# Sums of the down weights in a pool of their own, and down-stage buffers in pools by first use

## The chip, the cores and the metric

The kernel runs on one core of a Trainium2 chip. A NeuronCore has TensorE (PE: matmuls, results in PSUM), VectorE (DVE), ScalarE (ACT), GpSimd (POOL) and SyncE (SP); here SP issues every DMA, in one queue in order. Each engine works through its own instruction list in order and waits for others by semaphores: an instruction that waits holds up everything behind it on its engine. The metric is the device time of one execution in microseconds (us), the median of several runs.

## The reference, cut to what matters

One layer over 128 context and 2048 latent tokens (2176 in all, width 1024), in float32:

```python
h = rmsnorm(x, norm1) * (1 + scale1) + shift1
sc_b, sc_c, sc_x, q, k, v, o, g = split(h @ w_in)
y_sc = sc_b * conv3(sc_c * sc_x)                 # short convolution
h_m = mlstm_bidir(q, k, v, g) normed * sigmoid(o)
x = x + gate1 * (concat(y_sc, h_m) @ w_out)
h2 = rmsnorm(x, norm2) * (1 + scale2) + shift2
a, gg = split(conv3(h2 @ w_up))
x = x + gate2 * ((silu(gg) * a) @ w_down)        # D_FF = 2816
y = rmsnorm(x, final_norm)
```

`shift`, `scale` and `gate` come from `silu(c) @ w_mod`.

## The kernel before, in words

Each float32 product is made of three matmuls: a value is split into a rounded high part and the rest (`wh`, `wl` for weights; `hH`, `hL` for activations), and `wh*hH + wh*hL + wl*hH` is summed in PSUM. ScalarE makes the high part, VectorE or GpSimd the rest.

Tokens are cut into six blocks of up to 384 (`BL`); group BB is blocks 3 to 5 (384, 384, 256), group BA blocks 0 to 2. The stages, in the order of the code:

1. Modulation for `norm1` on TensorE (`mod_pe`), then value projection and gates of BB (`vg`), then k and q of BB (`heads`), then the short convolution of BB (`shortconv`). For each of its four `m` and each block it has three gemms of 24 matmuls: `wc`, whose result ScalarE copies to `cr` (L388); `wx`, which VectorE multiplies into `cr` (L391); ScalarE starts `yr` (L393), VectorE adds two taps (L398, L400); `wb`, which VectorE multiplies into `yr` (L404). Each gemm takes one of four PSUM tiles `acc`; the tile is free again when the copy or product has read it.
2. Beside it runs the generator `side`: statistics of BA, the rest of the modulation (`mod_dve`: 32 rows of 512 KB, each multiplied twice on VectorE, L515, added at L517) and `down_sums`. The last makes four sums of quarter blocks of `w_down` (Strassen-like: the down stage uses 7 products in place of 8) and stores them to DRAM (`wsD`). It has 8 steps; a step loads four tiles of 128 x 704 float32 (352 KB each, L546), does four VectorE operations (L550 to L553) and stores four tiles (L556). The tiles are `wm` of the pool `start`, 5 buffers, which `mod_dve` uses too.
3. The output gate of BB and the normalisation of BA. The pool `start` is closed here; the next pools on its side (`ml`, `gt`, later `mb`) lie on its bytes.
4. Value projection and gates of BA (`run(vg(BA, ...))`), then `gate_phase` in the pool `gt`, woven with k of BA; then the pool `mb` is opened and the mLSTM scan runs (`weave`), with the rest of the projections and the output projection as filling; then the up stage (two halves, 22 column pairs, seven products each, on the slots `t6, t0, t1, t5, t2, t4, t3` in that order); then the down stage.
5. The down stage opens two pools: `dw` (weights: `st` 2 buffers, `wh` and `wl` 6 each) and `db` (activations: `us` 2, `cur` one for each of six parts, `bh` and `bl` 3 each of three widths), and starts with the loads of `cur` (L1038), their split into `bh` and `bl` (L1066, L1067) and that of the first weights (L1024 to L1028); the products are L1137 to L1139.

What sets the order of the instructions: the code is written as if it were sequential, and a planner then issues, for each engine, the ready instruction that stands first in the code, by its own estimate of when things are ready. An instruction written late but ready early can go out early. Pools with `side="right"` are laid from the top of SBUF downward in the order in which they are opened; a pool that is opened on bytes of closed pools has to wait for them.

Sizes per partition, from the tile shapes: `wh` or `wl` or `st` of the down stage 3072 bytes; `bh`, `bl` or `cur` 4352, 4352 and 3264 for the three parts; `us` 4352.

Of the kernel before, what the change touches and what calls it, by code (L numbers as in the profile page):

```python
# [18 lines left out]
P = 128  # L19
# [38 lines left out]
def hymba_kernel(ctx: ExitStack, tc: tile.TileContext, I, O):  # L58
# [42 lines left out]
    def run(g, side=None, every=1):  # L101
        for i, _ in enumerate(g):
            if side and i % every == 0:
                next(side, None)
# [209 lines left out]
    with ExitStack() as ph1:  # L314
# [21 lines left out]
        def load_vg(j):  # L336
            return [load_w(I["w_vg"][j, kk], WN) for kk in range(2)]

        def vg(blocks, hs, ws):
            for b in blocks:  # L340
                hH, hL = hs[b]
                for j in range(2):
                    for c in chunks(b):
                        o = c * P - BL[b][0]
                        acc = acc_tile()
                        for k in range(KT):
                            w_h, w_l = (x[:, (k % 4) * 264:(k % 4 + 1) * 264] for x in ws[2 * j + k // 4])
                            a_h, a_l = hH[:, k, o:o + P], hL[:, k, o:o + P]
                            PE.matmul(acc[:, :264], a_h, w_h, start=(k == 0), stop=False)
                            PE.matmul(acc[:, :264], a_h, w_l, start=False, stop=False)  # L350
                            PE.matmul(acc[:, :264], a_l, w_h, start=False, stop=(k == KT - 1))
                        r = rq.tile([P, 2, 129], F32, name="rv", bufs=4)
                        G.memset(r[:, :, 128:129], 1.0)
                        S.activation(r[:, :, :P], acc[:, :256].rearrange("p (h d) -> p h d", h=2), AF.Copy)
                        Q.dma_start(vD[c][:, 2 * j:2 * j + 2], r)
                        V.tensor_add(gates[:, c, j * 8:(j + 1) * 8], acc[:, 256:264],
                                     bgate[:, j * 8:(j + 1) * 8])
                        yield
# [107 lines left out]
        with tc.tile_pool(name="start", bufs=1, side="right") as stp:  # L466
# [41 lines left out]
            def mod_dve():  # L508
                for mt in range(16, 48):
                    st = stp.tile([P, 1024], F32, name="wm", bufs=5)  # L510
                    Q.dma_start(st, I["w_modr"][mt - 16])
                    t = stp.tile([P, 2], F32, name="mt", bufs=2)
                    for v in range(2):
                        jk = pm.tile([P, 2, 512], F32, name="y")
                        V.scalar_tensor_tensor(jk.rearrange("p a b -> p (a b)"), st, 1.0, cB[:, v], op0=ALU.mult, op1=ALU.mult,  # L515
                                               accum_out=t[:, v:v + 1])
                    V.tensor_scalar(modT[:, mt, :], t, bmod[:, mt:mt + 1], None, op0=ALU.add)  # L517
                    if mt == 39:
                        affine(1, 0, KT)
                    yield  # L520
# [10 lines left out]
            def first_stats():  # L531
                for b in BA:
                    ss = squares(b, load_x(b, I["x"], xp, "xt", 2))
                    yield
                    inv_rms(ss, BL[b][1], rcol(b))
                    yield

            def down_sums():

                n = KH * P // 2  # L540
                for m in range(4):
                    for q in range(2):
                        t = []
                        for mm, o in ((m + 4, n * 2), (m + 4, 0), (m, 0), (m, n * 2)):
                            x = stp.tile([P, 1024], F32, name="wm", bufs=5)
                            Q.dma_start(x[:, :n], I["w_down"][mm][:, o + q * n:o + (q + 1) * n])  # L546
                            t.append(x[:, :n])
                        yield
                        a22, a21, a11, a12 = t
                        V.tensor_add(a22, a21, a22)  # L550
                        V.tensor_sub(a21, a11, a21)
                        V.tensor_sub(a11, a22, a11)
                        V.tensor_sub(a12, a12, a11)  # L553
                        yield
                        for i, x in enumerate((a22, a11, a21, a12)):
                            Q.dma_start(wsD[i, m][:, q * n:(q + 1) * n], x)  # L556

            late()
            side = chain(first_stats(), mod_dve(), down_sums())
            run(vg((3,), hs, ws), prep(4))  # L560
            run(vg((4,), hs, ws), prep(5))
            run(vg((5,), hs, ws))
# [7 lines left out]
                hs[b] = make_h(b, I["x"], 0)  # L570

        ml = phr.enter_context(tc.tile_pool(name="ml", bufs=1, side="right"))


        WG, EM, AC = range(3)
# [143 lines left out]
        class Sums:  # L719
# [5 lines left out]
            def load(self):  # L725
                self.k2, self.v2 = load2(ml, "k2", kD, self.c + 1, self.hp), load_v(self.c + 1, self.hp)
# [133 lines left out]
                    next(fill, None)  # L860


        run(vg(BA, hs, load_vg(0) + load_vg(1)))
        with tc.tile_pool(name="gt", bufs=1, side="right") as gt:
            gph = gate_phase()
            kh = heads(BA, hs, 16, kD, AF.Copy, 1.0)
            while True:
                try:
                    next(gph)
                except StopIteration as e:  # L870
                    cols, colc, decB = e.value
                    break
                next(kh, None)
                next(kh, None)
            run(kh)
        php.close()
        del pas[1]
        pm = phr.enter_context(tc.tile_pool(name="pm1", bufs=1, space=PSUM))
# [131 lines left out]
    CK = ((0, 4), (4, 8), (8, KH))  # L1010
    PN = 2 * NB
    with ExitStack() as ph3:
        dw = ph3.enter_context(tc.tile_pool(name="dw", bufs=6, side="right"))
        db = ph3.enter_context(tc.tile_pool(name="db", bufs=3, side="right"))
        pd = ph3.enter_context(tc.tile_pool(name="pd", bufs=6, space=PSUM))

        def weights_d(i, m):
            n = KH * P
            w = [I["w_down"][m][:, :n], wsD[0, m], wsD[1, m], I["w_down"][m + 4][:, n:], I["w_down"][m][:, n:],
                 wsD[2, m], wsD[3, m]][i]  # L1020
            ws = []
            for a, e in ((0, 6 * P), (6 * P, n)):
                st = dw.tile([P, 6 * P], F32, name="st", bufs=2)
                Q.dma_start(st[:, :e - a], w[:, a:e])  # L1024
                wh = dw.tile([P, 6 * P], F32R, name="wh")
                wl = dw.tile([P, 6 * P], F32R, name="wl")
                S.activation(wh[:, :e - a], st[:, :e - a], AF.Copy)
                V.tensor_sub(wl[:, :e - a], st[:, :e - a], wh[:, :e - a].bitcast(F32))  # L1028
                ws.append((wh, wl))
            return ws  # L1030
# [31 lines left out]

        def parts(x, c):
            n = (CK[c][1] - CK[c][0]) * NB
            bh, bl = (db.tile([P, n], F32R, name=f"{k}{c}") for k in ("bh", "bl"))
            S.activation(bh, x, AF.Copy)  # L1066
            V.tensor_sub(bl, x, bh.bitcast(F32))  # L1067
            return bh, bl
# [177 lines left out]
```

## Time and profile before

| | |
|---|---|
| median of 3 runs | 2571.15 us (2570.41 to 2572.16) |
| profiled execution: time, span | 2569.87 us, 2568.1 us |
| TensorE, VectorE, ScalarE, GpSimd busy | 96%, 64%, 43%, 22% of the span |
| mean granted TensorE clock | 0.985 |
| DMA | 444.60 MB, mean 173 GB/s |

The span is from the first to the last instruction; busy shares are of the span. A busy TensorE is not TensorE at its peak. In a row of the timeline the brackets at the end hold the idle time of the engine before the instruction and what ended it.

### The profile page before, as it was taken

The page shows a single profiled execution, that of the slowest core. Times are in us where ns is not written, and L with a number is a line of the kernel's source. Part 1 is how long each engine was busy: PE and PEld are TensorE (multiplying, and loading weights), DVE is VectorE, ACT ScalarE, POOL GpSimd, SP SyncE. Part 2 cuts the span into 40 slices and gives each one's busy share as a digit, 9 for nine tenths or more (in the row PEclk, how much of TensorE's full clock was granted, in tenths as well). Part 3 has the DMA queues.
Part 4 walks back from the last instruction along what each step waited for, and adds up shares of the span by engine and source line. Part 5 has one row for each costly group of instructions (what it writes and reads, how often), then busy time and mean ns, then how long its engine had stood idle before and what let it go on. Part 6 is the DMA issues. An engine that isn't in the chain of part 4 may idle for free.

```text
span 2568.1 us, 42559 instructions
## 1 busy us (share of the span) xinstructions
PE 2469.4 (96%) x16127; PEld 2364.4 (92%) x16127; DVE 1644.1 (64%) x2741; ACT 1112.4 (43%) x2035; POOL 567.0 (22%) x470
## 2 busy tenths in 40 slices
PE   8997999999999889999999999899999989999998
PEld 7997999999999889889999999788888889999998
DVE  3995432322356565778678666877777786687676
ACT  4511133322245554455455444655555554444342
POOL 2542223211134333422112111221221200000000
PEclk9998999999999999999999999999999999999999
DMA  8788623356467787785225222422222286767674
GB/s 282 252 266 287 217 83 121 129 175 184 128 192 242 244 250 239 243 280 172 73 74 180 82 82 82 138 107 83 92 98 83 82 255 213 243 208 226 186 217 134
DMA packets 281423, 444.60 MB, mean 173 GB/s; under 512 B 23282, under 2 KB 206722, under 8 KB 279554
## 3 DMA queue, kind: packets, MB, share of 16 engines
q1 hardware_dynamic: 281218, 441.88, 53.1%
q8 instruction: 127, 2.08, 0.3%
q14 instruction: 78, 0.64, 0.1%
HBM read 335.31 MB, written 106.48 MB: 172 GB/s over the span
## 4 chain that ended last, share of the span: by engine, by line
PE 64%; DMA 6%; DVE 5%; issue 2%; ACT 2%; POOL 1%; SPq 0%; DVEq 0%; ACTq 0%; POOLq 0%
PE pa L979 6%; PE pa L981 6%; PE pa L980 6%; PE d L1138 5%; PE d L1139 5%; PE d L1137 5%; PE acc L204 4%; PE acc L206 4%; PE acc L205 4%; PE pb L979 3%; PE pb L981 3%; PE pb L980 3%; PE pc L979 2%; PE pc L980 2%; PE pc L981 2%
## 5 line engine op out<-in xcount | busy, mean ns | idle before, releaser
L204 PE MATMUL acc<-hH,wh 128*128 128x384 f32 (+1 forms) x1536 | 515.8, 336 | 23.3 <-DVE cr L391 9.9
L206 PE MATMUL acc<-hH,wl 128*128 128x384 f32 (+1 forms) x1536 | 506.5, 330 | 0.0
L205 PE MATMUL acc<-hL,wh 128*128 128x384 f32 (+1 forms) x1536 | 506.3, 330 | 0.0
L1137 PE MATMUL d<-bh,wh 128*128 128x272 f32 x1232 | 357.3, 290 | 6.5 <-ACT bh L1066 6.5
L1138 PE MATMUL d<-bl,wh 128*128 128x272 f32 x1232 | 357.6, 290 | 0.7 <-DVE bl L1067 0.7
L1139 PE MATMUL d<-bh,wl 128*128 128x272 f32 x1232 | 357.8, 290 | 0.0
L979 PE MATMUL pa<-tH,wh 128*128 128x288 f32 (+1 forms) x1056 | 347.9, 329 | 3.9 <-DVE raw L993 1.9
L981 PE MATMUL pa<-tH,wl 128*128 128x288 f32 (+1 forms) x1056 | 346.3, 328 | 1.0 <-DVE wl L294 1.0
L980 PE MATMUL pa<-tL,wh 128*128 128x288 f32 (+1 forms) x1056 | 346.6, 328 | 0.0
L294 POOL TENSOR_TENSOR wl<-st,wh 128x512 fp32r<-128x512 f32 x132 | 184.6, 1399 | 700.0 <-ACT wh L293 656.0
L113 POOL TENSOR_TENSOR wl<-wst,wh 128x512 fp32r<-128x512 f32 (+1 forms) x160 | 235.7, 1496 | 467.6 <-ACT wh L110 455.5
L204 PEld LDWEIGHTS acc<-hH,wh 128*128 128x128 f32 x1536 | 292.6, 191 | 26.6 <-DVE cr L391 11.0
L205 PEld LDWEIGHTS acc<-hL,wh 128*128 128x128 f32 x1536 | 292.8, 191 | 0.0
L206 PEld LDWEIGHTS acc<-hH,wl 128*128 128x128 f32 x1536 | 292.2, 190 | 0.2 <-issue 0.2
L924 DVE SCALAR_TENSOR_TENSOR tt<-raw,fw,tt 128x127 f32<-128x127 f32 (+4 forms) x264 | 245.2, 949 | 4.8 <-ACT tt L930 3.8
L1137 PEld LDWEIGHTS d<-bh,wh 128*128 128x128 f32 x1232 | 233.4, 190 | 7.0 <-ACT bh L1066 6.9
L1138 PEld LDWEIGHTS d<-bl,wh 128*128 128x128 f32 x1232 | 233.6, 190 | 1.2 <-DVE bl L1067 1.0
L1139 PEld LDWEIGHTS d<-bh,wl 128*128 128x128 f32 x1232 | 233.5, 190 | 0.0
L979 PEld LDWEIGHTS pa<-tH,wh 128*128 128x128 f32 x1056 | 198.2, 188 | 20.9 <-ACT c L986 2.6
L981 PEld LDWEIGHTS pa<-tH,wl 128*128 128x128 f32 x1056 | 198.8, 188 | 17.0 <-DVE wl L294 1.4
L980 PEld LDWEIGHTS pa<-tL,wh 128*128 128x128 f32 x1056 | 198.5, 188 | 15.6
L293 ACT ACTIVATE wh<-s 128x512 fp32r<-128x512 f32 x176 | 110.8, 630 | 177.8 <-PE pc L980 96.8
(235 smaller groups left out, 4840.3 us busy)
## 6 DMA issues: line engine op xcount, KB each, us to landing
st<-in_w_up SPq DMA_DIRECT2D x88, 512.0 KB, 4.4
us<-uD SPq DMA_DIRECT2D x48, 544.0 KB, 4.8
wst<-in_w_in SPq DMA_DIRECT2D x48, 512.0 KB, 4.3
uD<-tt SPq DMA_DIRECT2D x44, 544.0 KB, 2.7
R<-nD SPq DMA_DIRECT2D x34, 512.0 KB, 5.5
wm<-in_w_modr SPq DMA_DIRECT2D x32, 512.0 KB, 4.8
wst<-in_w_out SPq DMA_DIRECT2D x24, 512.0 KB, 4.9
st<-wsD SPq DMA_DIRECT2D x32, 384.0 KB, 3.4
```

Source lines behind the costliest of these rows:

```text
L113: G.tensor_sub(wl[:, a:a + n // 2], st[:, a:a + n // 2], wh[:, a:a + n // 2].bitcast(F32))
L204: PE.matmul(acc[:, :n], w_h, hH[:, k, :n], start=(k == 0), stop=False)
L205: PE.matmul(acc[:, :n], w_h, hL[:, k, :n], start=False, stop=False)
L206: PE.matmul(acc[:, :n], w_l, hH[:, k, :n], start=False, stop=(k == KT - 1))
L294: (G if on_pool else V).tensor_sub(wl, a, wh.bitcast(F32))
L924: V.scalar_tensor_tensor(o, i, w, o, op0=ALU.mult, op1=ALU.add)
L979: PE.matmul(acc, wh[:, w], rh, start=(kk == 0 and i in (0, 1, 5)), stop=False, skip_group_check=True)
L980: PE.matmul(acc, wh[:, w], rl, start=False, stop=False, skip_group_check=True)
L981: PE.matmul(acc, wl[:, w], rh, start=False, stop=(kk == 3), skip_group_check=True)
L1137: PE.matmul(acc, wh[:, c], uh, start=(kk == 0), stop=False)
L1138: PE.matmul(acc, wh[:, c], ul, start=False, stop=False)
L1139: PE.matmul(acc, wl[:, c], uh, start=False, stop=(kk == KH - 1))
```

## The change

`down_sums` leaves the generator `side` and the pool `start`. It is written anew with a pool of its own, `dsp`, opened after `ml`: four tile names of two buffers each (22,528 bytes per partition), each step's loads written one step ahead of its sums. Its steps are taken one by one beside the value projection of BA, the gate phase and k of BA; `dsp` is closed ahead of `mb`. The loads, sums and stores are the same in number and size.

In the down stage `dw` and `db` become seven pools, opened in the order `dw0` (`st` 2, `wh` 2, `wl` 2), `db0` (`bh`, `bl` of the three widths), `db` (`us` 2, the six `cur`), `db1`, `db2`, `dw1`, `dw2`; weights and activation sets take turns over three pools where they took turns over the buffers of one. The sum of the bytes is the same.

```diff
--- before.py
+++ after.py
@@ -535,28 +535,8 @@
                     inv_rms(ss, BL[b][1], rcol(b))
                     yield
 
-            def down_sums():
-
-                n = KH * P // 2
-                for m in range(4):
-                    for q in range(2):
-                        t = []
-                        for mm, o in ((m + 4, n * 2), (m + 4, 0), (m, 0), (m, n * 2)):
-                            x = stp.tile([P, 1024], F32, name="wm", bufs=5)
-                            Q.dma_start(x[:, :n], I["w_down"][mm][:, o + q * n:o + (q + 1) * n])
-                            t.append(x[:, :n])
-                        yield
-                        a22, a21, a11, a12 = t
-                        V.tensor_add(a22, a21, a22)
-                        V.tensor_sub(a21, a11, a21)
-                        V.tensor_sub(a11, a22, a11)
-                        V.tensor_sub(a12, a12, a11)
-                        yield
-                        for i, x in enumerate((a22, a11, a21, a12)):
-                            Q.dma_start(wsD[i, m][:, q * n:(q + 1) * n], x)
-
             late()
-            side = chain(first_stats(), mod_dve(), down_sums())
+            side = chain(first_stats(), mod_dve())
             run(vg((3,), hs, ws), prep(4))
             run(vg((4,), hs, ws), prep(5))
             run(vg((5,), hs, ws))
@@ -570,6 +550,37 @@
                 hs[b] = make_h(b, I["x"], 0)
 
         ml = phr.enter_context(tc.tile_pool(name="ml", bufs=1, side="right"))
+        phd = ExitStack()
+        dsp = phd.enter_context(tc.tile_pool(name="dsp", bufs=2, side="right"))
+
+        def down_sums():
+
+            n = KH * P // 2
+            todo = [(m, q) for m in range(4) for q in range(2)]
+
+            def load(m, q):
+                t = []
+                for i, (mm, o) in enumerate(((m + 4, n * 2), (m + 4, 0), (m, 0), (m, n * 2))):
+                    x = dsp.tile([P, n], F32, name=f"a{i}")
+                    Q.dma_start(x, I["w_down"][mm][:, o + q * n:o + (q + 1) * n])
+                    t.append(x)
+                return t
+
+            t = load(*todo[0])
+            yield
+            for k, (m, q) in enumerate(todo):
+                nt = load(*todo[k + 1]) if k < 7 else None
+                yield
+                a22, a21, a11, a12 = t
+                V.tensor_add(a22, a21, a22)
+                V.tensor_sub(a21, a11, a21)
+                yield
+                V.tensor_sub(a11, a22, a11)
+                V.tensor_sub(a12, a12, a11)
+                yield
+                for i, x in enumerate((a22, a11, a21, a12)):
+                    Q.dma_start(wsD[i, m][:, q * n:(q + 1) * n], x)
+                t = nt
 
 
         WG, EM, AC = range(3)
@@ -860,7 +871,8 @@
                     next(fill, None)
 
 
-        run(vg(BA, hs, load_vg(0) + load_vg(1)))
+        dsums = down_sums()
+        run(vg(BA, hs, load_vg(0) + load_vg(1)), dsums)
         with tc.tile_pool(name="gt", bufs=1, side="right") as gt:
             gph = gate_phase()
             kh = heads(BA, hs, 16, kD, AF.Copy, 1.0)
@@ -872,7 +884,10 @@
                     break
                 next(kh, None)
                 next(kh, None)
-            run(kh)
+                next(dsums, None)
+            run(kh, dsums)
+        run(dsums)
+        phd.close()
         php.close()
         del pas[1]
         pm = phr.enter_context(tc.tile_pool(name="pm1", bufs=1, space=PSUM))
@@ -1010,20 +1025,26 @@
     CK = ((0, 4), (4, 8), (8, KH))
     PN = 2 * NB
     with ExitStack() as ph3:
-        dw = ph3.enter_context(tc.tile_pool(name="dw", bufs=6, side="right"))
-        db = ph3.enter_context(tc.tile_pool(name="db", bufs=3, side="right"))
+        def right(name, bufs=1):
+            return ph3.enter_context(tc.tile_pool(name=name, bufs=bufs, side="right"))
+
+        dw, bslot = [right("dw0", 2)], [right("db0")]
+        db = right("db")
+        bslot += [right("db1"), right("db2")]
+        dw += [right("dw1", 2), right("dw2", 2)]
+        wturn, bturn = count(), count()
         pd = ph3.enter_context(tc.tile_pool(name="pd", bufs=6, space=PSUM))
 
         def weights_d(i, m):
             n = KH * P
             w = [I["w_down"][m][:, :n], wsD[0, m], wsD[1, m], I["w_down"][m + 4][:, n:], I["w_down"][m][:, n:],
                  wsD[2, m], wsD[3, m]][i]
-            ws = []
+            ws, pool = [], dw[next(wturn) % 3]
             for a, e in ((0, 6 * P), (6 * P, n)):
-                st = dw.tile([P, 6 * P], F32, name="st", bufs=2)
+                st = dw[0].tile([P, 6 * P], F32, name="st")
                 Q.dma_start(st[:, :e - a], w[:, a:e])
-                wh = dw.tile([P, 6 * P], F32R, name="wh")
-                wl = dw.tile([P, 6 * P], F32R, name="wl")
+                wh = pool.tile([P, 6 * P], F32R, name="wh")
+                wl = pool.tile([P, 6 * P], F32R, name="wl")
                 S.activation(wh[:, :e - a], st[:, :e - a], AF.Copy)
                 V.tensor_sub(wl[:, :e - a], st[:, :e - a], wh[:, :e - a].bitcast(F32))
                 ws.append((wh, wl))
@@ -1062,7 +1083,8 @@
 
         def parts(x, c):
             n = (CK[c][1] - CK[c][0]) * NB
-            bh, bl = (db.tile([P, n], F32R, name=f"{k}{c}") for k in ("bh", "bl"))
+            pool = bslot[next(bturn) // 3 % 3]
+            bh, bl = (pool.tile([P, n], F32R, name=f"{k}{c}") for k in ("bh", "bl"))
             S.activation(bh, x, AF.Copy)
             V.tensor_sub(bl, x, bh.bitcast(F32))
             return bh, bl
```

## Rows read from the trace of the kernel before

**Rows 1.** The page: busy us of an engine, share of the span, instructions.
```profile
PE 2469.4 (96%) x16127; PEld 2364.4 (92%) x16127; DVE 1644.1 (64%) x2741; ACT 1112.4 (43%) x2035; POOL 567.0 (22%) x470
```
**Rows 2.** Waits of TensorE: who waited for whom, us in total, times, longest.
```profile
PE acc L204 <- DVE cr L391: 9.9, 3, 8.1
...
PE d L1137 <- ACT bh L1066: 6.5, 1, 6.5
```
**Rows 3.** Stretches: us from:to, length, busy of each engine, clock, DMA.
```profile
204.00:218.00 14.00, 6.20 (x36) 5.87 (x34) 4.49 (x6) 0.00 (x0) 0.00 (x0) 0.80 0.85 287
218.00:230.00 12.00, 7.84 (x34) 7.53 (x35) 5.25 (x8) 1.08 (x2) 0.00 (x0) 0.78 0.95 353
230.00:250.00 20.00, 18.70 (x118) 18.29 (x118) 11.68 (x16) 4.85 (x7) 6.50 (x5) 0.93 0.90 307
250.00:290.00 40.00, 39.08 (x247) 38.88 (x247) 18.02 (x24) 6.18 (x10) 10.68 (x8) 1.00 0.84 299
...
395.00:450.00 55.00, 53.42 (x416) 53.00 (x415) 12.81 (x36) 17.66 (x35) 17.75 (x28) 0.97 0.29 96
```
**Rows 4.** Timeline of VectorE, 196 to 341 us: start, duration, line, operation, tiles.
```profile
199.87 1.97 DVE L551 TENSOR_TENSOR wm<-wm 128x704 f32<-128x704 f32 x1
...
203.72 0.21 DVE L517 TENSOR_SCALAR modT<-mt,bmod 128x2 f32<-128x2 f32 x1
...
214.13 0.89 DVE L550 TENSOR_TENSOR wm<-wm 128x704 f32<-128x704 f32 x1 [9.41 <-DMA wm<-in_w_down]
...
217.71 0.55 DVE L391 TENSOR_TENSOR cr<-acc,cr 128x384 f32<-128x384 f32 x1
...
306.61 0.42 DVE L391 TENSOR_TENSOR cr<-acc,cr 128x256 f32<-128x256 f32 x1 [5.22 <-PE acc L206]
...
317.87 0.56 DVE L391 TENSOR_TENSOR cr<-acc,cr 128x384 f32<-128x384 f32 x1 [6.74 <-PE acc L206]
...
340.42 0.42 DVE L391 TENSOR_TENSOR cr<-acc,cr 128x256 f32<-128x256 f32 x1 [5.23 <-PE acc L206]
```
**Rows 5.** Timeline of TensorE, 188 to 219 us.
```profile
188.99 0.44 PE L204 MATMUL acc<-hH,wh 128*128 128x384 f32 x1 [0.34 <-ACT row L364]
...
218.32 0.69 PE L204 MATMUL acc<-hH,wh 128*128 128x384 f32 x1 [8.12 <-DVE cr L391]
```
**Rows 6.** Loads of line 546: duration ns min/median/max, first and last start.
```profile
L546 SPq DMA_DIRECT2D wm<-in_w_down x32: 327/397/1525, 188.6 to 275.7; - x32
```
**Rows 7.** Timeline of the DMA queue of SP, at four places.
```profile
290.05 0.31 SPq L637 DMA_DIRECT2D sm<-in_state_m  x1
...
496.71 0.82 SPq L886 DMA_DIRECT2D sf<-in_state  x2
...
2049.71 0.33 SPq L1024 DMA_DIRECT2D st<-in_w_down  x1
...
2063.75 0.38 SPq L1038 DMA_DIRECT2D cur<-uD  x1
```
**Rows 8.** DMA issues: count, KB each, median us from issue to landing.
```profile
wm<-in_w_down SPq DMA_DIRECT2D x32, 352.0 KB, 4.4
wsD<-wm SPq DMA_DIRECT2D x32, 352.0 KB, 2.7
```
**Rows 9.** Two more stretches, as in rows 3; the last number is GB/s.
```profile
220.00:224.00 4.00, 4.00 (x17) 4.00 (x17) 0.00 (x0) 0.00 (x0) 0.00 (x0) 0.67 1.02 404
...
2070.20:2076.00 5.80, 5.07 (x21) 4.76 (x22) 5.80 (x6) 5.27 (x6) 0.00 (x0) 0.50 1.04 329
```
**Rows 10.** Timeline of GpSimd, 196 to 202 us.
```profile
196.98 4.11 POOL L113 TENSOR_TENSOR wl<-wst,wh 128x512 fp32r<-128x512 f32 x2 [12.36 <-ACT wh L110]
```
**Rows 11.** Timeline of TensorE, the first matmul of the down stage.
```profile
2070.14 0.60 PE L1137 MATMUL d<-bh,wh 128*128 128x272 f32 x1 [6.47 <-ACT bh L1066]
```
**Rows 12.** Groups of lines 1027 and 1028: count, busy us, mean ns of one.
```profile
L1028 DVE TENSOR_TENSOR wl<-st,wh 128x768 fp32r<-128x768 f32 x56 | 53.7, 960 | 27.8 <-ACT wh L1027 27.3
L1027 ACT ACTIVATE wh<-st 128x768 fp32r<-128x768 f32 x56 | 47.3, 844 | 84.2 <-PE d L1138 46.7 <-DMA st<-in_w_down 20.0 <-DMA st<-wsD 12.1
```

## The prediction

> **What bounds the kernel now.** I read the page first: TensorE is busy for 2469.4 of 2568.1 us [rows 1], so only its idle places and its slow places can be won. Then its waits by releaser [rows 2]: the change can touch two of them, the gemms' wait for `cr` L391 (VectorE, 8.1 us at once) and the one wait of 6.5 us for `bh` L1066 at the start of the down stage. Then a table of stretches [rows 3]: between 204 and 290 us TensorE idles 7.80 + 4.16 + 1.30 + 0.92 = 14.2 us, with DMA up to 353 GB/s and a granted clock of 0.80 and 0.78 in the first two; between 395 and 450 us, where the change writes the sums, VectorE is busy for 12.8 of 55 us and DMA moves 96 GB/s.
>
> The cause of the first place stands in VectorE's order [rows 4]. The first block's convolution starts on TensorE at 188.99 [rows 5], and a gemm takes (218.32 - 8.12 - 188.99)/5 = 4.24 us, so the second gemm `wx` is ready at 197.5. Its product L391, which frees a PSUM tile, runs only at 217.71: in front of it stand the end of the modulation work (203.9) and the second step of `down_sums`, which waits 9.41 us for its loads. TensorE has four such tiles, goes three gemms further and stops at 210.2 for 8.1 us. What the whole episode costs: one `m` of the convolution takes 340.42 - 306.61 = 33.81 us, and from its first block to its third 340.42 - 317.87 = 22.55 [rows 4]; undisturbed, the last product would be due at 197.5 + 3 x 33.81 + 22.55 = 321.5, and it comes at 340.42. So 18.9 us are lost: 14.2 idle and 4.7 at the lower of the clock's two levels (1.2 GHz) after the idle stretches. That is all that moving the sums can win here.
>
> **The sums, part by part.** Removed from `start`: 32 loads and 32 stores of 352 KB [rows 8] and 32 VectorE operations of 0.89 us [rows 4] (28.5 us). The same number is added in `dsp`: no transfer and no operation goes away. What changes is where they stand and how many buffers they have (two sets of four for one set and a fifth).
>
> Where they will stand is the first choice. In the code they move from shortconv's last `m` (317.87) to the value projection (395 on). But the order of issue isn't the order of the code: the loads of `down_sums`, written some 120 us further down, go out from 188.6 on, as soon as `wm` buffers are free [rows 6]; and the load of `sm`, written in the gate phase behind the value projection, goes at 290.05 [rows 7], when `start` is let go. The new sums wait for nothing but the memory of `start`, whose last reader is now the modulation work. So I expect them not at 395 but right after that work: at 203.9 less the three sums that stood between its instructions (two of 0.89 and one of 1.97, which overlap their neighbours a little, so 3.5 [rows 4]), at 200.4, again beside the first blocks of the convolution, and with lower priority than it.
>
> Then the times. One step moves 8 x 352 KB = 2.88 MB, at 404 GB/s [rows 9] 7.1 us. Eight loads go out at once from 200.4; a lone load lands in 4.4 us [rows 8], so the first set is there at 205 and the first step ends at 205 + 3.6 = 208.6; the second set is there at about 209.4 and its step ends at 213. In the order of before two steps stand ahead of the first product, and I take two again: a third needs a store and a load (2.7 + 4.4 us) behind the first. The product then comes at 213.5 in place of 217.7, and TensorE stands 3.3 us in place of 8.1. Further on steps three to eight follow at 7.1 us each, two to a block: 14.2 us against 12.6 (3 x 4.2) of gemms, so the second and third block lose about 1 us each. That makes 5.3 us idle, with the clock's share as before (4.7/14.2) 7.1. The loads of `k2`, `v2` and `sb` (nine, some 1.2 MB, 3 us at 404 GB/s) now go out here too, as `start` is freed sooner; I add 2.4. Back: 9.5 us. Won: 18.9 - 9.5 = 9.4. The ends: nothing back (18.9 won), or each further step ahead of the first product costing 7.1 us.
>
> The queues that are passed: a load that waits for a store holds SP, and behind it stand `wst` and the `yD` stores; before, such waits were as many and what TensorE waited for was VectorE [rows 2], so nothing is counted. `mb` now waits for the last store from `dsp` too; its first load goes at 496.71 [rows 7], the sums end before 290 in my reckoning, and even from 395 on (23.1 MB, 57 us at 404 GB/s) they would end some 44 us ahead of it.
>
> The trace shows one thing more: the sum at 199.87 took 1.97 us beside a POOL operation [rows 10], where others take 0.89 [rows 4]. The Trainium skill (SBUF — State Buffer, Who interferes with whom) says why: a VectorE operation with two SBUF inputs contends with a GpSimd operation that reads SBUF. The row agrees. By that rule eight sums that all met POOL would put the first product 8 x 1.08 = 8.6 us later, and the stall would be near that of before: 2571, the end of rival 2 by another way. In 204 to 290 us POOL is busy for 17 of 86 us [rows 3], so I count two sums, inside the 2.4 above.
>
> **The down buffers.** By the shapes, the slots of the up stage and its pools lie from the top down: slot 6 (18,432 bytes), `fpool` (20,736), slot 0 (18,432), `fp` (30,720, to 88,320). Before, `dw` takes 43,008 and `db` the next 104,448. A new pool waits until all older pools under its whole range are free: `sf`, read from an input alone, goes out only at 496.71, when the gate tiles are done, though it shares no byte with them; only its pool does. So `st` goes at 2049.71, when the last gemm on slot 0 is done, and `cur` at 2063.75, when the last gemm of all is done [rows 7]. After: `dw0` (18,432) lies on slot 6 alone, 2.8 us sooner (five gemm stages lie between 2049.71 and 2063.75); `db0` (to 42,368) on `fpool` and slot 0; but `db` with `cur` (to 75,008) still lies on `fp`, whose last wh and wl are read by the last gemm. The chain from `cur` at 2063.75 over bh to the first gemm at 2070.14 [rows 11] stays. The second weights now wait for slot 4 (one stage before the end) and their conversions come nearer to bh and bl: I take +1 us. Bounds: -9.4 if `cur` were free at 2049.7 (the wait of 6.47 [rows 11], and half of the 5.8 us to 2076 at a clock of 0.50 [rows 9]); +3.6 for two conversions (0.84 on ACT and 0.96 on VectorE each [rows 12]) in front of bh and bl.
>
> **Sum.** -9.4 + 1 = -8.4 on the profiled execution's 2569.87 us (span 2568.1) = 2561.5; the median of the runs is 1.28 higher, so 2562.7, say 2563.
>
> The page DMA: Bandwidth & Descriptors of the Trainium skill (Where 436 GB/s comes from) gives about 358 GB/s as what binds between HBM and SBUF. The row of 404 doesn't agree. By the page a step would take 8.1 us and the estimate be about 2 us later, 2565.
>
> **Rivals.**
> 1. The stall goes wholly, because the sums run where they are written, in the 42 us that VectorE has free between 395 and 450. For it: nothing there would wait. Against it: the loads issued ahead of their place [rows 6, 7]. 2571 - 18.9 + 1 = 2553. Chance 0.14.
> 2. It stays: three steps stand ahead of the first product, 7.1 us more come back (16.6 of 18.9). For it: in the order of before VectorE already ran 20 us behind its due places (217.71 for 197.5 [rows 4, 5]), so what is due just after the product can as well be due before it. 2570. Chance 0.29.
> 3. Slower. With two sets the first loads need no store, so the planner can fit more steps into the same gap: from four steps ahead of the first product on, 9.5 + 14.2 = 23.7 us come back, more than was lost. Five make 30.8: +11.9 + 1, 2584. For it: all loads wait for one event now; against it: a set must be stored before its next load. Place: VectorE's queue before L391. Chance 0.14.
> 4. My forecast, 2558 to 2567: 0.43.
>
> Faster by over 0.2% (about what a measurement tells from no change here, 5.1 us) means below 2566.0: most of case 4 (0.36), all of case 1, a little of 2 (0.04): 0.54. Slower, above 2576.3: 0.11 of case 3 and 0.03 of 2: 0.14. Same: 0.32. The range leaves out half of case 1 and the far half of case 3: 2553 to 2578.
>
> **What would show it.** Right: sums on VectorE between 204 and 265, two steps ahead of the first L391, that at 212 to 215, TensorE idle between 204 and 290 for about 5 us in place of 14.2, `cur` within 0.5 us of the last up gemm. Wrong: sums after 395 (case 1), three or more steps ahead of L391 (2 and 3), `cur` issued before the last gemm, or a change of over 3 us between 300 and 2040 us, where I count nothing.

## The result and the profile after

Before 2570.52 us (median of 16 runs), after 2577.58 us (16 runs): ratio 1.0031, 95% interval 1.0021 to 1.0040. The change makes the kernel slower, by 7 us between the medians and by 8.0 us (5.4 to 10.3 of 2570) by the ratio; 2563 was forecast. The profiled execution of the changed kernel (2571.69 us, span 2569.9) is the lowest of its 16 runs, so its span stands only 1.8 us above the one before, and the loss has to be read in its stage.

Line numbers have moved: the loads of the sums are L565, the sums L575 to L579, their stores L582; L391 and L404 are as before. Waits of TensorE (who waited for whom: us in total, times, longest), to be held against [rows 2]:

```profile
PE acc L204 <- DVE cr L391: 15.2, 4, 9.0
...
PE d L1159 <- ACT bh L1088: 6.7, 1, 6.7
```

The wait for L391 was to shrink and has grown from 9.9 to 15.2 us; the wait for `bh` is unchanged. The same stretches as in [rows 3] (length, busy PE, PEld, DVE, ACT, POOL, clock, DMA share, GB/s):

```profile
204.00:218.00 14.00, 6.64 (x38) 6.31 (x37) 6.06 (x7) 0.00 (x0) 0.00 (x0) 0.85 0.99 356
218.00:230.00 12.00, 9.46 (x49) 9.14 (x50) 6.71 (x10) 1.08 (x2) 0.00 (x0) 0.75 0.91 333
230.00:250.00 20.00, 13.26 (x73) 12.76 (x72) 9.22 (x9) 2.87 (x4) 6.68 (x4) 0.83 0.75 245
250.00:290.00 40.00, 37.02 (x234) 36.62 (x233) 19.22 (x30) 6.65 (x10) 8.34 (x6) 1.00 0.79 270
```

TensorE idles 7.36 + 2.54 + 6.74 + 2.98 = 19.6 us here; before it was 14.2. The first stretch is no worse than before; the third is the new loss (6.74 for 1.30), and there DMA moves less than before (245 for 307 GB/s), so it isn't the transfers that are short of room. VectorE, in order of time (start, duration, line, operation, tiles, idle before and what ended it), beside [rows 4]:

```profile
202.60 0.23 DVE L517 TENSOR_SCALAR modT<-mt,bmod 128x2 f32<-128x2 f32 x1
...
208.51 0.89 DVE L575 TENSOR_TENSOR a<-a,a 128x704 f32<-128x704 f32 x1 [5.48 <-DMA a<-in_w_down]
211.91 0.89 DVE L576 TENSOR_TENSOR a<-a,a 128x704 f32<-128x704 f32 x1 [2.50 <-DMA a<-in_w_down]
...
215.01 0.89 DVE L575 TENSOR_TENSOR a<-a,a 128x704 f32<-128x704 f32 x1 [0.36 <-DMA a<-in_w_down]
...
219.03 0.55 DVE L391 TENSOR_TENSOR cr<-acc,cr 128x384 f32<-128x384 f32 x1
...
224.66 0.89 DVE L575 TENSOR_TENSOR a<-a,a 128x704 f32<-128x704 f32 x1 [3.04 <-DMA a<-in_w_down]
...
235.14 0.89 DVE L575 TENSOR_TENSOR a<-a,a 128x704 f32<-128x704 f32 x1 [6.47 <-DMA a<-in_w_down]
...
238.43 1.98 DVE L578 TENSOR_TENSOR a<-a,a 128x704 f32<-128x704 f32 x1
241.88 1.95 DVE L579 TENSOR_TENSOR a<-a,a 128x704 f32<-128x704 f32 x1
...
249.33 0.89 DVE L575 TENSOR_TENSOR a<-a,a 128x704 f32<-128x704 f32 x1 [5.04 <-DMA a<-in_w_down]
...
266.34 0.89 DVE L575 TENSOR_TENSOR a<-a,a 128x704 f32<-128x704 f32 x1 [9.66 <-DMA a<-in_w_down]
...
286.87 0.89 DVE L575 TENSOR_TENSOR a<-a,a 128x704 f32<-128x704 f32 x1 [3.77 <-DMA a<-in_w_down]
...
348.15 0.42 DVE L391 TENSOR_TENSOR cr<-acc,cr 128x256 f32<-128x256 f32 x1 [5.23 <-PE acc L206]
```

Two steps stand ahead of the first product, as forecast, but that product runs at 219.03, later than before (217.71). From the third step on each waits for its loads (3.04, 6.47, 5.04, 9.66 ...), and in each of the first six blocks a product, L391 or L404, stands behind such a step. TensorE's first wait is no shorter than before ([rows 5]: 8.12 us):

```profile
219.64 0.69 PE L204 MATMUL acc<-hH,wh 128*128 128x384 f32 x1 [9.00 <-DVE cr L391]
```

The last product, L391 at 348.15, comes 7.7 us later than before (340.42): here the loss is seen. Of the 7.7 us 1.3 stand at the first product (219.03 for 217.71); the rest arises behind it. The third step is level with that of before, the eighth is 9.5 us later; the rows of before:

```profile
224.89 0.89 DVE L550 TENSOR_TENSOR wm<-wm 128x704 f32<-128x704 f32 x1 [5.24 <-DMA wm<-in_w_down]
...
277.38 1.58 DVE L550 TENSOR_TENSOR wm<-wm 128x704 f32<-128x704 f32 x1 [2.16 <-DMA wm<-in_w_down]
```

The DMA queue of SP says why the loads are late:

```profile
187.45 0.90 SPq L365 DMA_DIRECT2D qD<-row  x2
202.86 0.81 SPq L565 DMA_DIRECT2D a<-in_w_down  x2
203.77 0.38 SPq L365 DMA_DIRECT2D qD<-row  x1
204.19 0.43 SPq L108 DMA_DIRECT2D wst<-in_w_in  x1
204.66 0.48 SPq L565 DMA_DIRECT2D a<-in_w_down  x1
...
238.78 0.33 SPq L565 DMA_DIRECT2D a<-in_w_down  x1
244.31 0.32 SPq L405 DMA_DIRECT2D yD<-yr  x1
244.72 1.36 SPq L565 DMA_DIRECT2D a<-in_w_down  x3
```

SP issues nothing between 188.35 and 202.86: the first load of the new pool waits for the last reader of the whole pool `start`, and all else waits behind it; before, the sums' loads went out one by one from 188.6 [rows 6]. Later the queues of SP and VectorE hold each other: at 238.78 one load of a step goes out, the other three stand behind a `yD` store until 244.31, that store waits for its product L404 on VectorE, and L404 stands behind sums there.

The down stage: `cur` is issued at 2066.13, 0.06 us after the end of the last up gemm (its last matmul starts at 2065.67 and takes 0.40), as before, and the first matmul waits for it as in [rows 11]:

```profile
2066.13 5.16 SPq L1059 DMA_DIRECT2D cur<-uD  x6
```
```profile
2072.77 0.59 PE L1159 MATMUL d<-bh,wh 128*128 128x272 f32 x1 [6.71 <-ACT bh L1088]
```

### The profile page after: what moved, and what is told of

Same layout as the page of the kernel before. It is cut to its first block, busy times and chain, and to the rows that moved or that the text cites. A ratio compares the mean times of both kernels' runs of the same rounds, so it can differ in the third digit from the quotient of the medians.

```text
span 2569.9 us, 42547 instructions
## 1 busy us (share of the span) xinstructions
PE 2469.0 (96%) x16127; PEld 2364.7 (92%) x16127; DVE 1648.1 (64%) x2741; ACT 1112.4 (43%) x2035; POOL 561.2 (22%) x470
## 4 chain that ended last, share of the span: by engine, by line
PE 62%; DMA 7%; DVE 6%; issue 2%; ACT 1%; POOL 1%; SPq 1%; DVEq 0%; POOLq 0%; ACTq 0%
PE pa L994 6%; PE pa L996 6%; PE pa L995 6%; PE d L1160 5%; PE d L1159 5%; PE d L1161 5%; PE acc L204 3%; PE acc L206 3%; PE acc L205 3%; PE pb L994 3%; PE pb L996 3%; PE pb L995 3%; PE pc L995 2%; PE pc L994 2%; PE pc L996 2%
## 5 line engine op out<-in xcount | busy, mean ns | idle before, releaser
L204 PE MATMUL acc<-hH,wh 128*128 128x384 f32 (+1 forms) x1536 | 517.2, 337 | 26.7 <-DVE cr L391 15.2
L995 PEld LDWEIGHTS pa<-tL,wh 128*128 128x128 f32 x1056 | 198.2, 188 | 15.4
```

The source lines that it names most:

```text
L204: PE.matmul(acc[:, :n], w_h, hH[:, k, :n], start=(k == 0), stop=False)
L995: PE.matmul(acc, wh[:, w], rl, start=False, stop=False, skip_group_check=True)
```

## The experiments

Each kernel was timed against the kernel before, interleaved on the same chip. "Last L391" is the start of the last product of the convolution in its profiled execution.

| kernel | ratio to before, 95% interval | that is, us of 2570 | last L391 |
|---|---|---|---|
| before | 1 | 0 | 340.42 |
| after | 1.0031 (1.0021 to 1.0040) | +8.0 | 348.15 |
| sums_only | 1.0023 (1.0006 to 1.0039) | +5.9 | 347.51 |
| down_only | 1.0000 (0.9987 to 1.0014) | 0.0 | 343.25 |
| one_set | 1.0040 (1.0025 to 1.0055) | +10.3 | 349.43 |
| before_held | 1.0015 (1.0003 to 1.0027) | +3.9 | 346.55 |
| sp_order | 0.9980 (0.9968 to 0.9992) | -5.1 | 334.01 |
| dve_order | 0.9958 (0.9947 to 0.9970) | -10.8 | 330.01 |
| paced | 0.9962 (0.9950 to 0.9974) | -9.8 | 330.07 |
| late | 0.9973 (0.9959 to 0.9987) | -6.9 | 322.92 |
| paced2 | 0.9940 (0.9926 to 0.9954) | -15.4 | 322.72 |
| before_ordered | 0.9936 (0.9922 to 0.9949) | -16.4 | 323.00 |
| db_first | 0.9982 (0.9968 to 0.9996) | -4.6 | 339.43 |
| paced2_dbf | 0.9908 (0.9890 to 0.9926) | -23.6 | 322.04 |

Where the sums stay in the convolution and `cur` isn't moved, the shift of the last product is the change of the time to within some 3 us. So much one execution differs from another: before, down_only and db_first have the same convolution, and their last products stand at 340.42, 343.25 and 339.43. What lies between that product and the first up gemm took 787.3 us before, 783.1 after, and 782.5 to 792.4 in the twelve others.

**Which part: sums_only and down_only.** In the first, `dw` and `db` are put back; in the second, the sums are.

> The changed sums, with the down stage's two pools as before. Theory (the whole loss of 7 us is the sums': VectorE's queue in order holds the convolution's products L391 and L404 behind sums that wait for loads, and the last product came 7.7 us later): about 2577.5 us, +7, with VectorE's last L391 of the convolution at about 348 us. Rival (the down pools lose it, the sums are neutral): 2570.5 us, no change from before.

> The sums as before, with the changed down-stage pools. Theory (the down pools change nothing: cur is still issued at the end of the last up gemm and the first down gemm waits 6.5 us for bh): 2570.5 us, within 1.5 of before. Rival (the down pools carry the loss): 2577.5 us, +7.

The sums carry the loss (+5.9, last product at 347.51, span 2575.6), the down pools carry nothing. Their interval of -3.3 to +3.6 us doesn't tell my +1 from 0.

**The sums where they are written: late.** The edit keeps an order of issue on a queue; it adds no wait for completion:

```diff
-                    Q.dma_start(x, I["w_down"][mm][:, o + q * n:o + (q + 1) * n])
+                    with tc.issue_after(vst[0]):
+                        Q.dma_start(x, I["w_down"][mm][:, o + q * n:o + (q + 1) * n])
```

(`vst[0]` is the latest `vD` store of the value projection.)

> The changed kernel, but each load of the sums is kept behind the latest vD store written before it on SP's queue, so that the sums run beside the value projection and gate phase of BA where they are written, after the convolution. Theory (the loss is the products' wait behind the sums in VectorE's queue during the convolution): no sums between 200 and 330 us, no stall of TensorE over 2 us there, the convolution's last L391 at 321 to 327 us instead of 348, and the time 2552 to 2558 us. Rival 1 (the sums hold VectorE's part of the value projection, the gates, as they held the products, and half comes back): 2562 to 2570 us. Rival 2 (the loss was not the order in the convolution): 2577 us.

VectorE's last product, and one of the windows where the sums now stand:

```profile
322.92 0.42 DVE L393 TENSOR_TENSOR cr<-acc,cr 128x256 f32<-128x256 f32 x1 [5.23 <-PE acc L206]
```
```profile
395.00:450.00 55.00, 47.45 (x352) 46.58 (x352) 27.33 (x71) 14.67 (x30) 4.45 (x12) 0.96 0.93 317
```

No wait of TensorE for anything is left between 204 and 350 us, and the last product comes at 322.92. So the undisturbed convolution ends there: before lost 17.5 us, after 25.2. But the time falls by 6.9 only, not by 17.5: in the new place TensorE is busy for 47.45 of 55 us where it was 53.42 [rows 3], with DMA at a share of 0.93. The longest of its waits there, one that before doesn't have, is for VectorE:

```profile
PE S L673 <- DVE mi L669: 4.9, 1, 4.9
```

These rows show only a part of what comes back: the profiled execution (2557.58 us) is the lowest of its 12 runs and 12.3 us below that of before. My expectation of 2552 to 2558 was wrong, its first rival right (2563.18).

**Order or traffic: paced, dve_order, sp_order.** The sums stay in the convolution, all of their 23 MB too; only the order of issue is set, in both queues or in one:

```diff
+        def behind(done, k):
+            return tc.issue_after(done[k]) if k > 0 or done is prod else ExitStack()
...
+                    with behind(yst, 2 * m + q - 1):
+                        Q.dma_start(x, I["w_down"][mm][:, o + q * n:o + (q + 1) * n])
...
+                with behind(prod, k):
+                    V.tensor_add(a22, a21, a22)
+                    V.tensor_sub(a21, a11, a21)
```

`yst` holds the `yD` stores and `prod` the products L404, both by block. The first `behind` is SP's order (paced, sp_order), the second VectorE's (paced, dve_order). Steps and blocks are counted from 0 here; the loads of steps 0 and 1 are left free, the others stand behind the store of block k-1.

> The changed kernel with the sums left in the convolution, the same traffic in the same stretch, but put in order by hand: the sums of step k stand in VectorE's queue behind the product L404 of block k, and the loads of step k behind the yD store of block k-1 on SP's queue, so that each load has a block (11.3 us) of lead. Theory (the loss is the order in VectorE's queue: a product behind a sum that waits): the convolution's last L391 at 322 to 326 us instead of 348, no wait of TensorE over 2.5 us between 205 and 340 us, 2552 to 2560 us (the lower end if nothing comes back later as it does when the sums stand at 379 to 474). Rival (the loss is the sums' 23 MB of traffic beside the convolution, which slows weights and stores whatever the order): last L391 at 335 us or later, 2568 to 2577 us.

> As the ordered version of the sums in the convolution, but only VectorE's order is set (sums of step k behind L404 of block k); SP's order stays the planner's. Theory (VectorE's queue is the place of the loss): nearly as good as with both, last L391 at 322 to 328 us, 2553 to 2562 us. Rival (SP's queue, in which a load that waits for a store holds weights and yD stores, carries half or more): last L391 at 335 us or later, 2566 us or more.

> Only SP's order is set (loads of step k behind the yD store of block k-1); VectorE's order is the planner's, which puts two steps ahead of the first product L391 as in the changed kernel, and later sums beside products. Theory (VectorE's queue): the first product stays at 217 to 219 us and TensorE's wait of 9 us with it, the later waits shrink or stay; 2566 to 2577 us. Rival (SP's queue): the time falls as far as with both orders, below 2560 us.

The traffic isn't the cause: with it in place, order alone turns +8.0 into -9.8. VectorE's order carries all of it (-10.8 alone); SP's alone gives 13.1 of the 17.8 us between after and paced (-5.1). What SP's order leaves is the first wait. In sp_order the first product still stands behind two steps, and of the 8.7 us that TensorE waits for such products between 190 and 350 us, 8.4 are the wait for this one:

```profile
219.85 0.55 DVE L393 TENSOR_TENSOR cr<-acc,cr 128x384 f32<-128x384 f32 x1
```
```profile
PE acc L204 <- DVE cr L393: 8.7, 2, 8.4
```

So the later waits go when either queue is put in order, and the first one only with VectorE's. The expectation for sp_order had this first wait right and the time wrong: 2563.60 us lies between the theory (2566 to 2577) and its rival (below 2560).

In paced and dve_order the last product (330.07, 330.01) is 7 us later than in the undisturbed case, and later than expected (up to 326 and 328); their times are 2560.45 and 2560.64. VectorE of paced shows what still stands ahead of the first product, and TensorE what it costs:

```profile
202.54 0.23 DVE L519 TENSOR_SCALAR modT<-mt,bmod 128x2 f32<-128x2 f32 x1
...
216.21 0.23 DVE L668 COPY mi<-sm 1x4 f32<-1x4 f32 x2 [13.24 <-DMA sm<-in_state_m]
216.35 0.54 DVE L393 TENSOR_TENSOR cr<-acc,cr 128x384 f32<-128x384 f32 x1
```
```profile
216.95 0.69 PE L204 MATMUL acc<-hH,wh 128*128 128x384 f32 x1 [6.96 <-DVE cr L393]
```

Two copies of four numbers, which the program has only in the gate phase, were issued ahead of the product, and they wait 13.24 us for a 32-byte load that stands on SP behind the eight loads of the sums.

**One set of buffers: one_set.** `bufs=2` of `dsp` becomes `bufs=1`.

> The changed kernel with one buffer of each of the four names in place of two. My prediction counted on the second set for a pace of 7.1 us a step, and the changed kernel makes 11.2 us. Theory (the pace is set by the transfers themselves and by SP's queue, 2.9 MB a step at some 260 GB/s, not by the buffers): a step every 11 to 13 us, 2574 to 2582 us. Rival (the second set carries the pace): a step every 15 us or more, the sums end after 320 us, 2585 us or more.

Slower than before by 10.3 us, which doesn't tell it from after (+8.0); its time, 2580.99 us, lies in the range of the theory. Its steps start at 209.4 to 305.5, some 13.7 us apart, where two sets made (286.87 - 208.51)/7 = 11.2. That is between the theory (11 to 13) and the rival (15 or more): the second set does shorten a step, but not to 7.1.

**The later start alone: before_held.** In the kernel before, one element of each tile of the first step is written by VectorE behind the last L517:

```diff
+                            if m + q == 0:
+                                with tc.issue_after(mod_end[0]):
+                                    V.memset(x[:, :1], 0.0)
                             Q.dma_start(x[:, :n], I["w_down"][mm][:, o + q * n:o + (q + 1) * n])
```

> The kernel before, in which the first four loads of the sums may not go out until the modulation work is done (a one-element write of their tile behind the last L517 on VectorE, about 203 us), as the new pool makes them wait in the changed kernel; before, they go out from 188.6 us. Nothing of pools or buffers is changed. Theory (what the change costs over before is this later start, since the sums keep their pace of 10.5 to 11 us a step and the products are tied to them): the last L391 of the convolution at 346 to 352 us instead of 340.4, 2576 to 2582 us. Rival (the cost lies in the new pool and its order, not in the start): last L391 at 341 us, 2570 to 2572 us.

```profile
190.72 0.91 SPq L365 DMA_DIRECT2D qD<-row  x2
205.53 0.81 SPq L551 DMA_DIRECT2D wm<-in_w_down  x2
```
```profile
226.12 0.55 DVE L391 TENSOR_TENSOR cr<-acc,cr 128x384 f32<-128x384 f32 x1
...
346.55 0.42 DVE L391 TENSOR_TENSOR cr<-acc,cr 128x256 f32<-128x256 f32 x1 [5.23 <-PE acc L206]
```
```profile
PE acc L204 <- DVE cr L391: 13.5, 1, 13.5
```

The same gap in SP's queue as after, and 3.9 us (0.8 to 6.9) of loss: in its direction as expected, in its size half. The 2576 to 2582 of the expectation would be +6 or more; the last product is in the expected range. But the loss stands in another place than after. Here it is one wait of 13.5 us for the first product, which comes at 226.12; after, with a second set of buffers, that product came at 219.03, 1.3 us later than before, and the loss arose behind it. So a later start costs the kernel before 3.9 us; that it is a part of what the change loses is not shown.

**The order mended: paced2 and before_ordered.** paced2 is paced with the two copies kept behind L404 of block 8 too. before_ordered is the kernel before, its pool `start` and five `wm` buffers kept, with the sums written after the convolution and the two orders set as in paced (but only step 0's loads are free). The edit of paced2 beside that of paced:

```diff
-                    V.tensor_copy(mi[:, d, c0, :], sm0[:, 4 * d:4 * d + 4])
+                    with tc.issue_after(prod[8]):
+                        V.tensor_copy(mi[:, d, c0, :], sm0[:, 4 * d:4 * d + 4])
```

> The ordered sums in the convolution, and the two copies of the gate phase that read the small load sm also kept behind a later product (L404 of block 8). In the ordered version they stood ahead of the first product and waited 13.24 us for sm, which stands behind the eight first loads of the sums; TensorE waited 7.0 us for that product. Theory: the first product at 206 us, no wait over 2 us, last L391 at 323 us, 7 us less than the ordered version: 2552 to 2555 us. Rival (the first loads hold something else too, weights or the yD stores, and the wait only passes on): last L391 at 328 us or later, 2558 to 2561 us.

> The kernel before, with its sums in the pool start and its five wm buffers, and only the order of issue set: sums of step k behind L404 of block k on VectorE, loads of step k behind the yD store of block k-1 on SP; the sums are written after the convolution. No new pool, no second set, the down stage as before. Theory (the order alone is the lever, the pool is not needed): the first product at about 204 us, last L391 at 323 to 328 us, 2550 to 2556 us. Rival (with five buffers the loads come too late behind the stores, and the products wait for sums again): last L391 at 332 us or later, 2560 us or more.

```profile
203.16 0.56 DVE L393 TENSOR_TENSOR cr<-acc,cr 128x384 f32<-128x384 f32 x1
...
209.19 0.89 DVE L582 TENSOR_TENSOR a<-a,a 128x704 f32<-128x704 f32 x1 [2.77 <-DMA a<-in_w_down]
...
292.76 0.92 DVE L582 TENSOR_TENSOR a<-a,a 128x704 f32<-128x704 f32 x1 [1.58 <-DMA a<-in_w_down]
...
322.72 0.43 DVE L393 TENSOR_TENSOR cr<-acc,cr 128x256 f32<-128x256 f32 x1 [5.23 <-PE acc L206]
```

Shown of paced2: the first product at 203.16, the last at 322.72, nothing clear of the noise given back later: -15.4 (2550.78 us, a little below the expected range, in a turn in which before took 2566.09). Its steps are still slow, (292.76 - 209.19)/7 = 11.9 us apart; standing behind the products, they cost nothing. The products of before_ordered are the same to 0.3 us (203.25 and 323.00), and its time, -16.4, isn't told from that of paced2. So the pool of their own wasn't needed to win this; the order was.

**The down stage: db_first and paced2_dbf.** The pool with `cur` is opened first, so that it lies on slot 6 and `fpool` and on no byte of `fp`; first with the sums of before, then with those of paced2.

```diff
+        db = right("db")
         dw, bslot = [right("dw0", 2)], [right("db0")]
-        db = right("db")
```

(The lines are those of the changed kernel.)

> The sums as before; the changed down-stage pools, but the pool with cur and us (32,640 bytes) is opened first, so that it lies on slot 6 and fpool alone and not on fp, which the last up gemm reads. Theory (cur is held by the pool under it, and the wait of 6.5 us for bh and the low clock after it hang on cur): cur is issued 10 us or more before the last up gemm, the wait for bh falls below 1 us, 2561 to 2564 us (-7 to -9). Rival 1 (cur waits for something else, the uD stores or the weights): cur within 1 us of the last up gemm as before, 2570.5 us. Rival 2 (the wait passes to the first weights, whose pool now lies lower): half of it, 2566 to 2568 us.

> The same, and with the pool of cur and us opened first in the down stage. Theory (the two gains lie in different stages and add): 4 to 6 us less than without, 2547 to 2550 us. Rival (they don't add: cur and its halves then meet other transfers): no less than 2552 us.

SP's queue, the first matmul and the stretch behind it in db_first, beside [rows 7, 9, 11]:

```profile
2051.63 0.98 SPq L1044 DMA_DIRECT2D cur<-uD  x2
```
```profile
2070.38 0.39 PE L1144 MATMUL d<-bh,wh 128*128 128x272 f32 x1 [2.19 <-ACT bh L1073]
```
```profile
2070.20:2076.00 5.80, 4.65 (x34) 4.45 (x35) 5.80 (x6) 5.80 (x8) 0.00 (x0) 1.00 0.37 124
```

The first two of the six `cur` go 16.6 us ahead of the last up gemm's end (2068.2), the wait falls from 6.47 to 2.19 us, and the clock behind it is 1.00 for 0.50. Worth 4.6 us (1.0 to 8.2) alone, against 7 to 9 expected, and the wait was to fall below 1 us: the time, 2567.20 us, lies in the range of the second rival (the wait passes to the first weights, 2566 to 2568). The trace goes with it: ScalarE makes the first `wh` at 2067.40, where it made it at 2053.29 before, and the first `bh` behind it at 2069.23, so what is waited for is no longer `cur`. On top of paced2, timed beside it, the same edit is worth (0.9940 - 0.9908) 8.2 us, where 4 to 6 were expected; the spread of the six runs of each (some 3 to 14 us) doesn't tell these apart. paced2_dbf is the fastest kernel here, 2542.02 us beside 2566.09.

## Why the prediction was wrong

Its steps in their order.

- **What the place costs: right.** 18.9 us were read as lost before; with the sums out of the way it is 17.5 (340.42 - 322.92). The due time worked out for the last product was 321.5.
- **The sums are issued right behind the modulation work, two steps ahead of the first product: right.** That work ended at 202.83, not at 200.4. The wait of TensorE behind it was to be 3.3 us and was 9.0.
- **"Eight loads go out at once from 200.4 ... the first set is there at 205": the first step that failed.** They went out from 202.86 to 211.3, among `qD` stores and weights that the waiting load had held, and the third tile was there at 211.9. The two steps then ended at 219.1 and not at 213: 2.4 us of this from the later start, 3.7 from the landing. From 204 to 218 us DMA was full (share 0.99) at 356 GB/s; the row of 404 was one of 4 us and was taken for more than it carries. At 356 GB/s a step's 2.88 MB would take 8.1 us, only 1.0 more than was reckoned. The Trainium skill (DMA: Bandwidth & Descriptors, Where 436 GB/s comes from) gives about 358 GB/s as what binds between HBM and SBUF; these 14 us agree with it, the 4 us of [rows 9] don't.
- **"Steps three to eight follow at 7.1 us each, two to a block": the step that cost most.** 7.1 is bytes over a rate. Measured from the third step to the eighth: (286.87 - 224.66)/5 = 12.4 us, one step to a block. The trace of before had the answer: its steps were (277.38 - 224.89)/5 = 10.5 us apart. A step is a circle: load, sums, store, and a later load (with two sets that of the step after next) waits for the store. The pace costs only through the products that stand behind the sums, as paced2 shows with steps of 11.9 us and no loss. The stores took 5.9 us to land where they took 2.7 [rows 8], the loads 5.0 for 4.4:

```profile
a<-in_w_down SPq DMA_DIRECT2D x32, 352.0 KB, 5.0
...
wsD<-a SPq DMA_DIRECT2D x32, 352.0 KB, 5.9
```

- **The 2.4 us for nine loads that "now go out here too": wrong in place.** `sb`, `k` and `v` went out behind the sums, some 10 us later than before (290.41) and not among the first blocks; only `sm` came sooner (273.61 for 290.05). No run shows what this term is worth:

```profile
300.61 1.88 SPq L898 DMA_DIRECT2D sb<-in_state  x2
```

- **"so nothing is counted" for SP's queue: wrong.** The circle goes through SP and VectorE, as the rows at 238.78 to 244.72 show: 6 us for one step. Setting SP's order alone moved the time by 13 us from after (+8.0 to -5.1).
- **9.5 us were to come back; 25.2 did.** This is the term that was mis-sized: -9.4 was +7.7 in the profiled executions.
- **The sums that meet GpSimd: right.** Two were counted and two did, 1.98 and 1.95 us for 0.89, both while GpSimd ran from 238.27 to 244.95.
- **The down buffers: right in place.** `cur` at the last gemm, the chain kept, about nothing gained or lost. The bound of -9.4 with `cur` free holds for db_first and paced2_dbf (-4.6 and -8.2), but 2.19 us of the wait stay, behind the weights' conversions, where the bound counted the whole.

Of the rivals, the third named the place, VectorE's queue ahead of L391, but not the way: not four steps ahead of the first product, but one step ahead of a product in each of the first six blocks; that its 23.7 us come near the 25.2 measured is luck. The first, 2553 with the sums at 395, held for the stall and not for the time (late: 2563.18), since the value projection and the gate phase then wait too. Shown is that the order in the two queues makes the loss: with it set, the same sums cost nothing. What is not settled is why the steps go round more slowly than before (12.4 us for 10.5): the later start, the later landing of the stores and the hold-ups in SP's queue were not tried apart in the changed kernel.

## What to carry to other kernels

Work that is only filling should stand behind the product of its block in every in-order queue it uses, with its load issued a block earlier; given that order, the same sums in the same place cost nothing (-16.4 us with no pool moved). Don't price a filling by bytes over bandwidth where load, work and store go round through two in-order queues: price the circle, by its pace in the trace of before where it runs there already (10.5 us here, not 7.1), and name what stands behind each of its waits. And look past the work that was moved: a pool that comes free sooner lets small things from far down the code slip ahead, and one 32-byte load kept TensorE waiting for 7 us.

## What was not expected of the hardware

A store of 352 KB landed in 2.7 us before and in 5.9 after, with the same number of stores in the same stage. In the eight kernels with two sets it is 5.2 to 6.6 us, in the five with the `wm` buffers 2.5 to 4.2, and in one_set, which differs from after in nothing else, 3.0. So the longer landing comes with the second set; by what way is not shown. And the clock at the start of the down stage stayed at 1.00 when TensorE's wait ahead of it was 2.19 us, and stood at 0.50 over the same stretch when it was 6.47.
